# A Strassen down projection whose sums are handed out in quarters behind the next product's steps

## The chip, the core and the metric

The kernel runs on one NeuronCore of a Trainium2 chip. The metric is device time in microseconds (us) of one execution of the whole layer; the figure of a kernel is the median of its runs.

## The reference, cut to what matters

A bidirectional encoder layer (a state-space branch and a windowed attention branch, merged, then a squared-ReLU MLP) is applied to two sequences of 512 rows with 1024 columns, all in fp32. The change lies in the last line, in the second product:

```python
def encoder_layer(x, bias, ..., w_out, ln2, w_up, w_down):
    ...
    x = x + mixed @ w_out
    h2 = rms_norm(x, ln2)
    return x + jnp.square(jax.nn.relu(h2 @ w_up)) @ w_down     # (1024 x 4096) @ (4096 x 1024)
```

## The kernel before

The kernel runs its stages one after another: projections, state-space branch, attention, gating and output projection, then the MLP's up projection and its down projection. The last of these starts at about 1154 us of the profiled span and runs to the end.

**The seven products.** Activations and weights of the down projection are cut into 2 x 2 blocks and multiplied by Strassen's scheme, seven block products in place of eight. The up projection leaves the seven left operands (blocks, sums and differences of them) in a scratch tensor in DRAM, `a_scr`. The seven right operands are made on the fly from three sets of tiles: `k1`, `k2` and `k3`, each of eight tiles `k1_0` to `k1_7` and so on (128 partitions x 1024 values). Two sets are combined into one by a subtraction on VectorE (L1509) when a product needs a difference of weight blocks. The products run in the order 1, 5, 6, 3, 7, 2, 4.

**One product.** `product_d(n)` takes four PSUM banks (512 columns each, one for each 128 output rows) out of eight, and goes over the inner dimension in eight steps. In each step SyncE's queue loads a left tile `d_a` (three buffers); ScalarE rounds the two operands to a high part (`a_hi`, `b_hi`, L1514); VectorE takes the low parts (`a_lo`, `b_lo`, L1515); TensorE does 24 matmuls (`mm3`: high x high at L116, low x high at L117, high x low at L118, for 2 row blocks and 4 banks). The `hi` and `lo` tiles have two buffers each, so ScalarE may round a step's operands once TensorE is done with the step two before.

**The end of a product.** The four banks of a finished product are copied or added into accumulators in SBUF: `q1`, `q3`, `q4`, `q5`, each 4 x 512 columns, one quarter `q1[:, t]` for each bank. The residual `x` is read back from DRAM in tiles `xq` of 4 x 512 columns. There is one `xq` buffer, so each of its four loads (L1525, on SyncE's queue) waits until the last sum that reads the previous one is done. Finished quarters go to DRAM (`store`, L1530). After product 1, L1534 copies the banks to `q1` on ScalarE and L1536 adds `xq` to them in one instruction over all four quarters (128x2048). After product 5, L1540 copies the banks to `q5`, L1541 makes `q4` by quarters, and L1543 adds `xq` to all of `q5`. After product 7, L1555 and L1556 add by quarters, and L1558 adds `xq` to all of `q1`.

**What sets the order.** No order is written out by hand in this stage. A scheduler gives each engine a fixed sequence when the program is built: it goes by the order in which the code issues instructions, and lets a later one pass where its own estimate of the times says that an earlier one isn't ready. Each engine then works through its sequence strictly in order, waiting at semaphores.

Of the kernel before, what the change touches and what calls it, by code (L numbers as in the profile page):

```python
# [63 lines left out]
def hybrid_layer(ctx, tc, x, rel, onehot, w_qkv, w_ug, vectors, lam, coefs, w_glu, w_out, ln2,  # L64
                 w_up, w_down, out):
    nc = tc.nc
    V, S, PE, GP, SP = nc.vector, nc.scalar, nc.tensor, nc.gpsimd, nc.sync
# [18 lines left out]
    def sps():  # L86
        return ps_s.tile([P, 512], F32, tag="sps", name="sps")
# [26 lines left out]
    def mm3(ps, a, b, first, last):  # L114

        PE.matmul(ps, a[0], b[0], start=first, stop=False)  # L116
        PE.matmul(ps, a[0], b[1], start=False, stop=False)  # L117
        PE.matmul(ps, a[1], b[0], start=False, stop=last)  # L118
# [159 lines left out]
    with tc.tile_pool(name="xin", bufs=1, reuse_waits="tile") as xin, tc.tile_pool(name="ssmc", bufs=1) as sc:  # L278
# [148 lines left out]
        ps = ps_o.tile([P, 512], F32, tag="po", name="line")  # L427
# [21 lines left out]
    with tc.tile_pool(name="hst", bufs=1) as hp:  # L449
# [147 lines left out]
        with tc.tile_pool(name="ssmo", bufs=2) as sp:  # L597
# [46 lines left out]
            for q in range(GROUPS // SH):  # L644
# [7 lines left out]
                ps = sps()  # L652
# [91 lines left out]
    with tc.tile_pool(name="att", bufs=2, reuse_waits="tile") as ap, tc.tile_pool(name="attc", bufs=1, reuse_waits="tile") as ac:  # L744
# [293 lines left out]
        with tc.manual_schedule(engines={ET.PE, ET.Activation, ET.DVE, ET.Pool}):  # L1038
            for i, (j, sq) in enumerate(steps):
# [4 lines left out]
                for qb in range(NB):  # L1044
                    if 1 <= i < 3:
                        t = (i - 1) * NB + qb
# [366 lines left out]
    def bank():  # L1413
        return ps_m.tile([P, HALF], F32, tag="bank", name="bank")
# [69 lines left out]
    with tc.tile_pool(name="downb", bufs=1, side="right", reuse_waits="tile") as db, \  # L1484
            tc.tile_pool(name="down", bufs=2, side="right", reuse_waits="tile") as dp, \
            tc.tile_pool(name="down0", bufs=2, side="right", reuse_waits="tile") as d0, \
            tc.tile_pool(name="downc", bufs=1, reuse_waits="tile") as dc:

        q5 = db.tile([P, 4, HALF], F32, name="q5")
        db.tile([P, HALF * 2], F32, name="apart")  # L1490
        k1 = [(d0 if r < 3 else db).tile([P, 2, HALF], F32, name=f"k1_{r}", bufs=1) for r in range(NPAIR // 2)]
        k2, k3 = [[dc.tile([P, 2, HALF], F32, name=f"k{i}_{r}") for r in range(NPAIR // 2)] for i in (2, 3)]
        q1, q3, q4 = [dc.tile([P, 4, HALF], F32, name=f"q{i}") for i in (1, 3, 4)]

        def product_d(n):

            ps = [bank() for _ in range(4)]
            for r in range(0, NPAIR, 2):
                rs = slice(r, r + 2)
                a = d0.tile([P, 2, HALF], F32, tag="d_a", name="d_a", bufs=3)  # L1500
                SP.dma_start(a, a_scr[n - 1, :, rs, :])
                new = {1: (k1, 0, 0), 5: (k2, 0, 1), 6: (k3, 1, 1), 2: (k3, 1, 0)}.get(n)
                if new:
                    SP.dma_start(new[0][r // 2], w_down[new[1], new[2], :, rs, :])
                b = {1: k1, 5: k1, 6: k1, 3: k3, 7: k2, 2: k3, 4: k1}[n][r // 2]
                if n in (5, 6, 7, 4):

                    p, q = {5: (k2, k1), 6: (k3, k1), 7: (k3, k2), 4: (k1, k3)}[n]
                    V.tensor_sub(b, p[r // 2], q[r // 2])  # L1509
                hl = []  # L1510
                for src, tag in ((a, "a"), (b, "b")):
                    hi = (d0 if tag == "a" else dp).tile([P, 2, HALF], F32R, tag=tag + "_hi", name=tag + "_hi")
                    lo = dp.tile([P, 2, HALF], F32R, tag=tag + "_lo", name=tag + "_lo")
                    S.copy(hi, src)  # L1514
                    V.tensor_sub(lo, src, hi.bitcast(F32))  # L1515
                    hl.append((hi, lo))
                for rr in range(2):
                    for t in range(4):
                        mm3(ps[t], [q[:, rr, t * P:(t + 1) * P] for q in hl[0]], [q[:, rr, :] for q in hl[1]],
                            r + rr == 0, r + rr == NPAIR - 1)  # L1520
            return ps

        def residual(sq, c):
            xq = dp.tile([P, 4, HALF], F32, tag="xq", name="xq", bufs=1)
            SP.dma_start(xq, x1_scr[sq * HALF:(sq + 1) * HALF, c * HALF:(c + 1) * HALF].rearrange("(t p) n -> p t n", p=P))  # L1525
            return xq

        def store(src, t, sq, c):
            row = sq * HALF + t * P
            SP.dma_start(out[row:row + P, c * HALF:(c + 1) * HALF], src)  # L1530

        ps = product_d(1)
        for t in range(4):
            S.copy(q1[:, t], ps[t])  # L1534
        xq = residual(0, 0)
        V.tensor_add(q3, q1, xq)  # L1536
        xq = residual(0, 1)
        ps = product_d(5)
        for t in range(4):
            S.copy(q5[:, t], ps[t])  # L1540
            V.tensor_add(q4[:, t], q5[:, t], xq[:, t])  # L1541
        xq = residual(1, 1)
        V.tensor_add(q5, q5, xq)  # L1543
        ps = product_d(6)
        for t in range(4):
            V.tensor_add(q1[:, t], ps[t], q1[:, t])
            V.tensor_add(q4[:, t], q1[:, t], q4[:, t])
        ps = product_d(3)
        for t in range(4):
            V.tensor_add(q4[:, t], ps[t], q4[:, t])  # L1550
            store(q4[:, t], t, 0, 1)
        xq = residual(1, 0)
        ps = product_d(7)
        for t in range(4):
            V.tensor_add(q1[:, t], ps[t], q1[:, t])  # L1555
            V.tensor_add(q5[:, t], q5[:, t], q1[:, t])  # L1556
            store(q5[:, t], t, 1, 1)
        V.tensor_add(q1, q1, xq)  # L1558
        ps = product_d(2)
        for t in range(4):  # L1560
            V.tensor_add(q3[:, t], ps[t], q3[:, t])
            store(q3[:, t], t, 0, 0)
        ps = product_d(4)
        for t in range(4):
            V.tensor_sub(q1[:, t], q1[:, t], ps[t])
            store(q1[:, t], t, 1, 0)
# [79 lines left out]
```

## Time and profile before

| what | value |
|---|---|
| median of 3 runs | 1475.15 us (1472.97 to 1476.32) |
| span of the profiled execution, first to last instruction | 1471.1 us |
| median less that span | 4.0 us |
| TensorE busy | 1442.0 us, 98% of the span |
| VectorE busy | 1092.2 us, 74% |
| ScalarE busy | 754.9 us, 51% |
| down projection, from its first matmul | about 1154 us to the end |

The profiled execution's own time is its span of 1471.1 us and what lies around it; the runs' median lies 4.0 us above that span. Times inside the profile are counted from the first instruction. "Idle before" is the time that an engine stood still before an instruction, and the arrow behind it names what it waited for. A row that ends in "x3" is three like instructions in a row, with their time from the first's start to the last's end.

### The profile page before, as it was taken

To read this page: it belongs to the slowest core of one execution; us is meant where nothing else is said; L and a number is where in the kernel's file an instruction comes from. 1 tells how busy PE (TensorE), PEld (TensorE's weight loads), DVE (VectorE), ACT (ScalarE), POOL (GpSimd) and SP (SyncE) were. 2 spreads that over 40 slices of the span, in tenths; PEclk is the share of its full clock that TensorE was granted. 3 is DMA by queue.
4 is the path that set the end of the run, shared out by engine and by line. 5 is a ranking of instruction groups with operands and counts; after the bars stand their busy time and mean duration, and the time that the engine had idled before them with its cause. 6 is when DMAs were issued, how large, how long until landed. Compare 5 with 4: busy or idle time off the path is not lost.

```text
span 1471.1 us, 22069 instructions
## 1 busy us (share of the span) xinstructions
PE 1442.0 (98%) x8074; PEld 1230.7 (84%) x8074; DVE 1092.2 (74%) x1965; ACT 754.9 (51%) x1346; POOL 226.8 (15%) x372
## 2 busy tenths in 40 slices
PE   6999999999999999999999999999999999999998
PEld 4888888888999999987888878888888878888787
DVE  7989849995446899988985587777776597475553
ACT  6678852234336888786343355454454444333332
POOL 3044451003332442252100000000000000000000
PEclk9999999999999999999999999999999999999999
DMA  4455559428630533345552255444442993454441
GB/s 177 137 165 174 159 157 339 144 100 288 234 135 24 172 104 106 105 150 177 182 192 102 86 169 174 149 146 154 145 146 108 339 330 103 158 184 147 126 130 58
DMA packets 98269, 234.48 MB, mean 159 GB/s; under 512 B 11722, under 2 KB 23242, under 8 KB 98160
## 3 DMA queue, kind: packets, MB, share of 16 engines
q1 hardware_dynamic: 59088, 135.35, 28.5%
q0 software_dynamic: 15744, 47.23, 9.9%
q10 hardware_dynamic: 23328, 50.47, 9.4%
q8 instruction: 64, 1.05, 0.3%
q14 instruction: 45, 0.37, 0.1%
HBM read 163.78 MB, written 80.77 MB: 166 GB/s over the span
## 4 chain that ended last, share of the span: by engine, by line
PE 74%; DVE 12%; DMA 4%; issue 4%; ACT 4%; POOL 2%; SPq 0%; DVEq 0%; ACTq 0%; POOLq 0%
PE bank L117 14%; PE bank L118 13%; PE bank L116 13%; PE acc L185 6%; PE acc L821 5%; PE acc L117 3%; PE acc L118 3%; PE acc L116 3%; PE acc L123 2%; DMA c_raw<-in_w_ug_dram 2%; PE sps L553 2%; PE po L904 2%; PE sps L872 2%; PE tps L888 2%; PE acc L225 1%
## 5 line engine op out<-in xcount | busy, mean ns | idle before, releaser
L185 PE MATMUL acc<-act,c_hi 128*128 128x512 f32 x768 | 244.2, 396 | 1.0 <-DVE act L311 1.0
L117 PE MATMUL bank<-b_lo,a_hi 128*128 128x512 f32 x448 | 174.6, 390 | 2.3 <-DVE b_lo L1515 2.3
L118 PE MATMUL bank<-b_hi,a_lo 128*128 128x512 f32 x448 | 174.3, 389 | 0.0
L116 PE MATMUL bank<-b_hi,a_hi 128*128 128x512 f32 x448 | 173.5, 389 | 0.0
L185 PEld LDWEIGHTS acc<-act,c_hi 128*128 128x128 f32 x768 | 143.0, 189 | 30.4 <-DVE act L311 2.4
L1514 ACT CAST a_hi<-d_a 128x1024 fp32r<-128x1024 f32 x56 | 59.0, 1054 | 180.5 <-PE bank L117 177.1
L185 PE MATMUL acc<-act,c_lo 128*128 128x512 f32 x384 | 151.0, 393 | 0.0
L116 PE MATMUL bank<-act,act 128*128 128x512 f32 x368 | 143.3, 389 | 0.5 <-ACT f_sum L1339 0.5
L117 PE MATMUL bank<-act,act 128*128 128x512 f32 x368 | 143.3, 389 | 0.2 <-DVE act L1298 0.2
L118 PE MATMUL bank<-act,act 128*128 128x512 f32 x368 | 143.2, 389 | 0.0
L1515 DVE TENSOR_TENSOR a_lo<-d_a,a_hi 128x1024 fp32r<-128x1024 f32 x56 | 68.5, 1224 | 98.5 <-ACT a_hi L1514 98.5
L821 PE MATMUL acc<-w_hi,act 128*128 128x256 f32 x512 | 114.1, 291 | 0.0
L117 PEld LDWEIGHTS bank<-b_lo,a_hi 128*128 128x128 f32 x448 | 84.1, 188 | 20.7 <-DVE b_lo L1515 3.3
L116 PEld LDWEIGHTS bank<-b_hi,a_hi 128*128 128x128 f32 x448 | 84.1, 188 | 17.6
L118 PEld LDWEIGHTS bank<-b_hi,a_lo 128*128 128x128 f32 x448 | 84.1, 188 | 17.4
L821 PEld LDWEIGHTS acc<-w_hi,act 128*128 128x128 f32 x512 | 87.1, 190 | 3.7
L185 PEld LDWEIGHTS acc<-act,c_lo 128*128 128x128 f32 x384 | 72.3, 188 | 14.7 <-DVE c_lo L176 0.4
L882 ACT ACTIVATE p<-p,nmx 128x257 f32<-128x257 f32 (+1 forms) x128 | 72.1, 564 | 19.7 <-DVE nmx L876 17.6
L116 PEld LDWEIGHTS bank<-act,act 128*128 128x128 f32 x368 | 69.1, 188 | 15.4 <-ACT f_sum L1339 0.9
L117 PEld LDWEIGHTS bank<-act,act 128*128 128x128 f32 x368 | 69.1, 188 | 14.8 <-DVE act L1298 0.5
L123 PE MATMUL acc<-act,gc_hi 128*128 128x512 f32 x256 | 81.2, 394 | 0.0
L118 PEld LDWEIGHTS bank<-act,act 128*128 128x128 f32 x368 | 69.1, 188 | 14.2
(333 smaller groups left out, 3425.1 us busy)
## 6 DMA issues: line engine op xcount, KB each, us to landing
d_a<-a_scr SPq DMA_DIRECT2D x56, 512.0 KB, 3.8
raws<-in_w_up_dram SPq DMA_DIRECT2D x32, 512.0 KB, 4.0
a_scr<-t ACTq DMA_DIRECT2D x64, 256.0 KB, 2.9
k<-in_w_down_dram SPq DMA_DIRECT2D x32, 512.0 KB, 5.9
c_raw<-in_w_ug_dram SPq DMA_DIRECT2D x48, 256.0 KB, 3.8
ct_scr<-ctab POOLq DMA_DIRECT2D x16, 512.0 KB, 4.7
ctab_in<-ct_scr POOLq DMA_DIRECT2D x16, 512.0 KB, 7.3
a_scr<-a ACTq DMA_DIRECT2D x32, 256.0 KB, 2.0
```

What stands on the lines that cost most here:

```text
L116: PE.matmul(ps, a[0], b[0], start=first, stop=False)
L117: PE.matmul(ps, a[0], b[1], start=False, stop=False)
L118: PE.matmul(ps, a[1], b[0], start=False, stop=last)
L123: PE.matmul(ps, w[wi][:, k, :], rows[yi], start=k + p == 0, stop=k == KT - 1 and p == 2)
L185: PE.matmul(ps, w[wi][:, k, :], hT[s][hi][:, k, :], start=n == 0, stop=n == 3 * KT - 1)
L553: PE.matmul(ps[:, i * P:(i + 1) * P], bm[:, ri, g, :], u_sb[:, gp * SH + g, :], start=True, stop=True)
L821: PE.matmul(self.ps, hT[sq][act][:, k, col:col + P], w[:, k % 4, :], start=i == 0, stop=i == 3 * KT - 1)
L872: PE.matmul(ps[:, 0:self.nk], qs, kk[:, self.k0 * P:self.k1 * P], start=i == 0, stop=i == 1)
L882: S.activation(p, p, AF.Exp, bias=self.nmx[:, h:h + 1], scale=-1.0, accum_out=self.sums[:, h, self.qb:self.qb + 1])
L888: PE.transpose(pt[:, h * P:(h + 1) * P], self.p[:, h, 1 + i * P:1 + (i + 1) * P], ident)
L1514: S.copy(hi, src)
L1515: V.tensor_sub(lo, src, hi.bitcast(F32))
```

## The change

The sums, copies and stores that follow a product become a function of the quarter `t`, and four such pieces are put in a list, `waiting`. The next product works the list off: one piece behind the instructions of each of its first four steps (`settle(1)`), and whatever is left behind its last. The three sums over 128x2048 (L1536, L1543, L1558) become four sums over 128x512 each. The load of a residual is now issued in the code behind the whole of the product whose sums use it. The seventh product's sums stay as they were.

```diff
+        waiting = []
+
+        def settle(n):
+            for _ in range(min(n, len(waiting))):
+                waiting.pop(0)()
...
                         mm3(ps[t], [q[:, rr, t * P:(t + 1) * P] for q in hl[0]], [q[:, rr, :] for q in hl[1]],
                             r + rr == 0, r + rr == NPAIR - 1)
+                settle(1)
+            settle(len(waiting))
             return ps
...
-        ps = product_d(1)
-        for t in range(4):
-            S.copy(q1[:, t], ps[t])
-        xq = residual(0, 0)
-        V.tensor_add(q3, q1, xq)
-        xq = residual(0, 1)
-        ps = product_d(5)
...
-        V.tensor_add(q5, q5, xq)
...
-        V.tensor_add(q1, q1, xq)
...
+        def later(fn, *args):
+            for t in range(4):
+                waiting.append(lambda t=t: fn(t, *args))
+
+        def first_out(t, ps, xq):
+            S.copy(q1[:, t], ps[t])
+            V.tensor_add(q3[:, t], q1[:, t], xq[:, t])
+
+        def second_out(t, ps, xq):
+            S.copy(q5[:, t], ps[t])
+            V.tensor_add(q4[:, t], q5[:, t], xq[:, t])
+
+        def third_out(t, ps, xq):
+            V.tensor_add(q1[:, t], ps[t], q1[:, t])
+            V.tensor_add(q4[:, t], q1[:, t], q4[:, t])
+            V.tensor_add(q5[:, t], q5[:, t], xq[:, t])
+
+        def fourth_out(t, ps):
+            V.tensor_add(q4[:, t], ps[t], q4[:, t])
+            store(q4[:, t], t, 0, 1)
+
+        def fifth_out(t, ps, xq):
+            V.tensor_add(q1[:, t], ps[t], q1[:, t])
+            V.tensor_add(q5[:, t], q5[:, t], q1[:, t])
+            store(q5[:, t], t, 1, 1)
+            V.tensor_add(q1[:, t], q1[:, t], xq[:, t])
+
+        def sixth_out(t, ps):
+            V.tensor_add(q3[:, t], ps[t], q3[:, t])
+            store(q3[:, t], t, 0, 0)
+
+        later(first_out, product_d(1), residual(0, 0))
+        later(second_out, product_d(5), residual(0, 1))
+        later(third_out, product_d(6), residual(1, 1))
+        later(fourth_out, product_d(3))
+        later(fifth_out, product_d(7), residual(1, 0))
+        later(sixth_out, product_d(2))
         ps = product_d(4)
```

Since the scheduler sets the sequence, the built programs say what moved. VectorE's sequence differs at four places, the heads of products 5, 6, 3 and 2; ScalarE's at two (products 5 and 6), TensorE's at two (the second steps of products 5 and 2, where the first high x high matmuls change places with the others), and SyncE's at one. The head of product 7 (the sums of `q4`) and that of product 4 (the sums of `q3`) keep their rows. In the rows below the operands stand with their buffer numbers.

**Place A, the head of product 5 (after product 1).** VectorE before; the first two rows are the low parts of product 5's step 0, and `k1_1` is the right operand of step 1:

```order
L1515 TENSOR_TENSOR a_lo_12296<-d_a_12291,a_hi_12295 128x1024
L1515 TENSOR_TENSOR b_lo_12300<-k1_0_11967,b_hi_12299 128x1024
L1509 TENSOR_TENSOR k2_2_11977<-k3_2_11985,k2_2_11977 128x1024
L1509 TENSOR_TENSOR k1_0_11967<-k3_0_11983,k1_0_11967 128x1024
L1509 TENSOR_TENSOR k2_3_11978<-k3_3_11986,k2_3_11978 128x1024
L1515 TENSOR_TENSOR a_lo_12332<-d_a_12327,a_hi_12331 128x1024
L1536 TENSOR_TENSOR q3_11992<-q1_11991,xq_12282 128x2048
L1515 TENSOR_TENSOR b_lo_12336<-k1_1_11968,b_hi_12335 128x1024
```

VectorE now (a line's number is higher in the changed file: L1515 has become L1521, L1509 has become L1515, L1536 has become L1546):

```order
L1521 TENSOR_TENSOR a_lo_12289<-d_a_12284,a_hi_12288 128x1024
L1521 TENSOR_TENSOR b_lo_12293<-k1_0_11967,b_hi_12292 128x1024
L1515 TENSOR_TENSOR k2_2_11977<-k3_2_11985,k2_2_11977 128x1024
L1546 TENSOR_TENSOR q3_11992<-q1_11991,xq_12278 128x512 x3
L1515 TENSOR_TENSOR k1_0_11967<-k3_0_11983,k1_0_11967 128x1024
L1521 TENSOR_TENSOR a_lo_12327<-d_a_12322,a_hi_12326 128x1024
L1521 TENSOR_TENSOR b_lo_12331<-k1_1_11968,b_hi_12330 128x1024
L1546 TENSOR_TENSOR q3_11992<-q1_11991,xq_12278 128x512
L1515 TENSOR_TENSOR k1_1_11968<-k3_1_11984,k1_1_11968 128x1024
L1515 TENSOR_TENSOR k2_3_11978<-k3_3_11986,k2_3_11978 128x1024
L1521 TENSOR_TENSOR a_lo_12365<-d_a_12360,a_hi_12364 128x1024
L1521 TENSOR_TENSOR b_lo_12369<-k1_2_11969,b_hi_12368 128x1024
```

Between the low parts of step 0 and `b_lo` of step 1 stood three weight subtractions, `a_lo` and the whole sum; now there are two subtractions, three quarters of the sum and `a_lo`. The last quarter and the subtraction of `k2_3` stand behind `b_lo`.

**Place B, the head of product 2 (after product 7).** VectorE before; `b_lo_13485` belongs to step 0, `b_lo_13520` to step 1:

```order
L1515 TENSOR_TENSOR b_lo_13485<-k3_0_11983,b_hi_13484 128x1024
L1555 TENSOR_TENSOR q1_11991<-bank_13176,q1_11991 128x512
L1555 TENSOR_TENSOR q1_11991<-bank_13177,q1_11991 128x512
L1556 TENSOR_TENSOR q5_11965<-q5_11965,q1_11991 128x512 x2
L1555 TENSOR_TENSOR q1_11991<-bank_13178,q1_11991 128x512
L1555 TENSOR_TENSOR q1_11991<-bank_13179,q1_11991 128x512
L1556 TENSOR_TENSOR q5_11965<-q5_11965,q1_11991 128x512 x2
L1515 TENSOR_TENSOR a_lo_13516<-d_a_13512,a_hi_13515 128x1024
L1558 TENSOR_TENSOR q1_11991<-q1_11991,xq_13174 128x2048
L1515 TENSOR_TENSOR b_lo_13520<-k3_1_11984,b_hi_13519 128x1024
```

VectorE now (L1555, L1556 and L1558 have become L1562, L1563 and L1565):

```order
L1521 TENSOR_TENSOR b_lo_13478<-k3_0_11983,b_hi_13477 128x1024
L1562 TENSOR_TENSOR q1_11991<-bank_13172,q1_11991 128x512
L1562 TENSOR_TENSOR q1_11991<-bank_13173,q1_11991 128x512
L1563 TENSOR_TENSOR q5_11965<-q5_11965,q1_11991 128x512 x2
L1565 TENSOR_TENSOR q1_11991<-q1_11991,xq_13464 128x512
L1521 TENSOR_TENSOR a_lo_13513<-d_a_13509,a_hi_13512 128x1024
L1521 TENSOR_TENSOR b_lo_13517<-k3_1_11984,b_hi_13516 128x1024
L1565 TENSOR_TENSOR q1_11991<-q1_11991,xq_13464 128x512
L1562 TENSOR_TENSOR q1_11991<-bank_13174,q1_11991 128x512
L1562 TENSOR_TENSOR q1_11991<-bank_13175,q1_11991 128x512
L1563 TENSOR_TENSOR q5_11965<-q5_11965,q1_11991 128x512 x2
L1521 TENSOR_TENSOR a_lo_13552<-d_a_13548,a_hi_13551 128x1024
```

The low parts of step 1 have moved ahead of half of the sums and of three quarters of the one over `xq`.

**Place C, the head of product 6 (after product 5).** VectorE before; `xq_12285` is the second residual and `xq_12587` the third, which goes into the same buffer:

```order
L1541 TENSOR_TENSOR q4_11993<-q5_11965,xq_12285 128x512 x3
L1515 TENSOR_TENSOR a_lo_12635<-d_a_12630,a_hi_12634 128x1024
L1541 TENSOR_TENSOR q4_11993<-q5_11965,xq_12285 128x512
L1515 TENSOR_TENSOR b_lo_12639<-k1_1_11968,b_hi_12638 128x1024
L1515 TENSOR_TENSOR a_lo_12671<-d_a_12666,a_hi_12670 128x1024
L1515 TENSOR_TENSOR b_lo_12675<-k1_2_11969,b_hi_12674 128x1024
L1543 TENSOR_TENSOR q5_11965<-q5_11965,xq_12587 128x2048
L1515 TENSOR_TENSOR a_lo_12707<-d_a_12702,a_hi_12706 128x1024
```

VectorE now (L1541 and L1543 have become L1550 and L1555):

```order
L1550 TENSOR_TENSOR q4_11993<-q5_11965,xq_12580 128x512 x3
L1521 TENSOR_TENSOR a_lo_12629<-d_a_12624,a_hi_12628 128x1024
L1521 TENSOR_TENSOR b_lo_12633<-k1_1_11968,b_hi_12632 128x1024
L1550 TENSOR_TENSOR q4_11993<-q5_11965,xq_12580 128x512
L1521 TENSOR_TENSOR a_lo_12667<-d_a_12662,a_hi_12666 128x1024
L1521 TENSOR_TENSOR b_lo_12671<-k1_2_11969,b_hi_12670 128x1024
L1555 TENSOR_TENSOR q5_11965<-q5_11965,xq_12882 128x512 x4
L1521 TENSOR_TENSOR a_lo_12705<-d_a_12700,a_hi_12704 128x1024
```

The last reader of the second residual, a quarter of `q4`, has gone behind `b_lo` of step 1, and the sum over the third residual is four instructions where it was one. At places A and C ScalarE's fourth bank copy has likewise gone from between `a_hi` and `b_hi` of step 1 to behind `b_hi`. On SyncE's queue, at place B, the four stores of `q5` are now two and two, with one load of `d_a` between.

More of the change, by code (lines that the diff above doesn't have):

```diff
@@ L1530, in store @@
             SP.dma_start(out[row:row + P, c * HALF:(c + 1) * HALF], src)
-        ps = product_d(1)
-        for t in range(4):
+        def later(fn, *args):
+            for t in range(4):
+                waiting.append(lambda t=t: fn(t, *args))
+        def first_out(t, ps, xq):
             S.copy(q1[:, t], ps[t])
-        xq = residual(0, 0)
-        V.tensor_add(q3, q1, xq)
-        xq = residual(0, 1)
-        ps = product_d(5)
-        for t in range(4):
+            V.tensor_add(q3[:, t], q1[:, t], xq[:, t])
+        def second_out(t, ps, xq):
             S.copy(q5[:, t], ps[t])
             V.tensor_add(q4[:, t], q5[:, t], xq[:, t])
[L1542 to L1545, printed above, removed]
+        def third_out(t, ps, xq):
             V.tensor_add(q1[:, t], ps[t], q1[:, t])
             V.tensor_add(q4[:, t], q1[:, t], q4[:, t])
-        ps = product_d(3)
-        for t in range(4):
+            V.tensor_add(q5[:, t], q5[:, t], xq[:, t])
+        def fourth_out(t, ps):
             V.tensor_add(q4[:, t], ps[t], q4[:, t])
             store(q4[:, t], t, 0, 1)
-        xq = residual(1, 0)
-        ps = product_d(7)
-        for t in range(4):
+        def fifth_out(t, ps, xq):
             V.tensor_add(q1[:, t], ps[t], q1[:, t])
@@ L1557, in hybrid_layer @@
             store(q5[:, t], t, 1, 1)
-        V.tensor_add(q1, q1, xq)
-        ps = product_d(2)
-        for t in range(4):
+            V.tensor_add(q1[:, t], q1[:, t], xq[:, t])
+        def sixth_out(t, ps):
             V.tensor_add(q3[:, t], ps[t], q3[:, t])
             store(q3[:, t], t, 0, 0)
+        later(first_out, product_d(1), residual(0, 0))
[4 more added lines that the diff above has]
+        later(sixth_out, product_d(2))
         ps = product_d(4)
```

## The prediction

> **What bounds the kernel now.** I read the page's busy times first, then the waits of TensorE, then the instructions in order of time around each wait.
>
> ```profile
> span 1471.1 us, 22069 instructions
> PE 1442.0 (98%) x8074; PEld 1230.7 (84%) x8074; DVE 1092.2 (74%) x1965; ACT 754.9 (51%) x1346; POOL 226.8 (15%) x372
> PE bank L117 <- DVE b_lo L1515: 2.3, 2, 1.2
> ```
>
> TensorE (PE) is busy for 98% of the span, so only work that TensorE itself waits for can move the end. The third row is from the waits asked for the down projection alone (930 us to the end), and it is the only row there: two waits, both of a low x high matmul for a `b_lo` that VectorE (DVE) makes. Whatever the change does to sums and copies, it can win no more than these two stops cost.
>
> What they cost shows in TensorE's own instructions. A step of 24 matmuls, undisturbed, runs from the first row to the second; the rows from 1208.55 are step 1 of product 5 up to the start of its step 2; those from 1384.15 are step 1 of product 2 up to its step 2.
>
> ```profile
> 1203.11 0.39 PE L116 MATMUL bank<-b_hi,a_hi 128*128 128x512 f32 x1
> 1208.55 0.84 PE L116 MATMUL bank<-b_hi,a_hi 128*128 128x512 f32 x3
> 1210.53 0.50 PE L117 MATMUL bank<-b_lo,a_hi 128*128 128x512 f32 x1 [1.14 <-DVE b_lo L1515]
> 1215.46 0.39 PE L116 MATMUL bank<-b_hi,a_hi 128*128 128x512 f32 x1
> 1384.15 1.07 PE L116 MATMUL bank<-b_hi,a_hi 128*128 128x512 f32 x4
> 1386.37 0.50 PE L117 MATMUL bank<-b_lo,a_hi 128*128 128x512 f32 x1 [1.15 <-DVE b_lo L1515]
> 1391.04 0.39 PE L116 MATMUL bank<-b_hi,a_hi 128*128 128x512 f32 x1
> ```
>
> A step takes 1208.55 - 1203.11 = 5.44 us, or 0.227 us for one matmul. The first disturbed step takes 6.91 and loses 1.47 us, the second takes 6.89 and loses 1.45. Together that is 2.92 us, more than the 2.3 of idle time, since a refilled pipeline is slow for one or two matmuls: at the first stop the fourth matmul was due at 1208.55 + 3 x 0.227 = 9.23 and came at 10.53, 1.30 late, so 0.17 of its 1.47 is refill.
>
> **The change part by part.** *Place A, the head of product 5.* Here are VectorE's rows before (DVE), then ScalarE's (ACT).
>
> ```profile
> 1201.38 1.22 DVE L1515 TENSOR_TENSOR b_lo<-k,b_hi 128x1024 fp32r<-128x1024 f32 x1
> 1202.51 3.49 DVE L1509 TENSOR_TENSOR k<-k,k 128x1024 f32<-128x1024 f32 x3
> 1205.92 1.22 DVE L1515 TENSOR_TENSOR a_lo<-d_a,a_hi 128x1024 fp32r<-128x1024 f32 x1
> 1207.05 2.28 DVE L1536 TENSOR_TENSOR q<-q,xq 128x2048 f32<-128x2048 f32 x1
> 1209.26 1.22 DVE L1515 TENSOR_TENSOR b_lo<-k,b_hi 128x1024 fp32r<-128x1024 f32 x1
> 1210.39 1.22 DVE L1509 TENSOR_TENSOR k<-k,k 128x1024 f32<-128x1024 f32 x1
> ...
> 1201.27 1.95 ACT L1534 COPY q<-bank 128x512 f32<-128x512 f32 x3 [1.62 <-PE bank L118]
> 1203.11 1.05 ACT L1514 CAST a_hi<-d_a 128x1024 fp32r<-128x1024 f32 x1
> 1204.06 0.58 ACT L1534 COPY q<-bank 128x512 f32<-128x512 f32 x1
> 1204.54 1.07 ACT L1514 CAST b_hi<-k 128x1024 fp32r<-128x1024 f32 x1
> ```
>
> The reader should see that from 1201.38 VectorE has no gap: this stop is VectorE's queue, five instructions long, and not ScalarE, whose `b_hi` was done at 1205.61. From start to start an instruction of 1024 columns takes 1.13 us and that of 2048 takes 2.21. A sum of 512 columns takes 0.60, from the two rows of L1555 and L1556 in place B below (1379.36 to 1380.56 to 1381.76, two instructions each).
>
> Now the same with the new order. Starting at 1202.51: `k2_2` 1.13, three quarters of `q3` 1.80, `k1_0` 1.13, `a_lo` 1.13; `b_lo` starts at 1207.70, ends 1.22 later at 1208.92, and with the 0.05 that lay before from its end (1210.48) to the matmul (1210.53) TensorE has it at 1208.97. ScalarE doesn't hold this up: the three copies are done at 1203.22, and the new order casts `b_hi` straight behind `a_hi`, half a microsecond sooner; the fourth copy slips to about 1205.6, and its quarter of `q3` isn't wanted before 1208.84. TensorE's sequence now puts one high x high matmul ahead of the first low x high, which is due at 1208.55 + 0.23 = 1208.78. So 0.19 is still late, with at most 0.17 of refill: 0.36 stays, and this place wins 1.11. Bounds: nothing stays (win 1.47), or the sums don't overlap at all and each takes its whole 0.69 (the L1541 row below), three times 0.09 more, so 0.63 stays (win 0.84). I take 0.36, from two consecutive sums on the same engine.
>
> The removed stop was also VectorE's time to catch up, so I followed its queue for three more steps. Step 2 has one quarter, `k1_1`, `k2_3`, `a_lo` before `b_lo`: 1208.84 + 0.60 + 3 x 1.13 = 1212.83, ready at 1214.10, wanted at 1214.58 (step 2 now starts at 1214.35). Step 3 has `k2_4`, `k1_2`, `k2_5`, `a_lo`: `b_lo` starts at 1218.48, ready at 1219.75, wanted at 1220.02. Step 4, with `k2_7` behind it now, is ready at 1224.3 and wanted at 1225.5. So there is no new stop, but at step 3 the margin is 0.27; if it fails, it costs what is missing and no more.
>
> *Place B, the head of product 2.* VectorE, then ScalarE, before:
>
> ```profile
> 1376.87 1.37 DVE L1555 TENSOR_TENSOR q<-bank,q 128x512 f32<-128x512 f32 x2 [0.18 <-PE bank L118]
> 1378.15 1.29 DVE L1556 TENSOR_TENSOR q<-q,q 128x512 f32<-128x512 f32 x2
> 1379.36 1.28 DVE L1555 TENSOR_TENSOR q<-bank,q 128x512 f32<-128x512 f32 x2
> 1380.56 1.29 DVE L1556 TENSOR_TENSOR q<-q,q 128x512 f32<-128x512 f32 x2
> 1381.76 1.22 DVE L1515 TENSOR_TENSOR a_lo<-d_a,a_hi 128x1024 fp32r<-128x1024 f32 x1
> 1382.89 2.29 DVE L1558 TENSOR_TENSOR q<-q,xq 128x2048 f32<-128x2048 f32 x1
> 1385.09 1.22 DVE L1515 TENSOR_TENSOR b_lo<-k,b_hi 128x1024 fp32r<-128x1024 f32 x1
> ...
> 1378.68 1.05 ACT L1514 CAST a_hi<-d_a 128x1024 fp32r<-128x1024 f32 x1 [3.43 <-PE bank L117]
> 1379.64 1.04 ACT L1514 CAST b_hi<-k 128x1024 fp32r<-128x1024 f32 x1
> 1384.12 1.06 ACT L1514 CAST a_hi<-d_a 128x1024 fp32r<-128x1024 f32 x1 [3.44 <-PE bank L117]
> ```
>
> Now two sums of L1555, two of L1556 and one quarter come first: 1379.36 + 0.60 = 1379.96; `a_hi` is there (1379.73). `a_lo` runs to 1381.09, `b_lo` is done by 1382.31, and TensorE wants it at 1384.15 + 0.23 = 1384.38: two microseconds to spare, so the whole 1.45 goes. What is late next? The deferred sums: one quarter, two of L1555, two of L1556, to 1385.2, behind them `a_lo` and `b_lo` of step 2, done by 1387.6, wanted at 1384.15 + 5.44 + 0.23 = 1389.8. The banks of product 7 come free by 1384.0 instead of 1380.6, but only product 4 wants them, a product later. On SyncE's queue the loads of `d_a` behind the last two stores of `q5` wait for sums that end at 1385.2; the first of them would wait in any case for its buffer, which `a_lo` of step 2 frees at about 1386.4. All of this costs nothing, with over 2 us of cover.
>
> *Place C, the head of product 6.* There was no stop here, and one could come:
>
> ```profile
> 1250.33 0.69 DVE L1541 TENSOR_TENSOR q<-q,xq 128x512 f32<-128x512 f32 x1
> 1250.93 1.22 DVE L1515 TENSOR_TENSOR b_lo<-k,b_hi 128x1024 fp32r<-128x1024 f32 x1
> 1258.34 2.29 DVE L1543 TENSOR_TENSOR q<-q,xq 128x2048 f32<-128x2048 f32 x1 [1.38 <-DMA xq<-x_scr]
> 1251.05 0.37 SPq L1525 DMA_DIRECT2D xq<-x_scr  x1
> 1264.42 0.39 PE L116 MATMUL bank<-b_hi,a_hi 128*128 128x512 f32 x1
> 1264.65 0.39 PE L117 MATMUL bank<-b_lo,a_hi 128*128 128x512 f32 x1
> DMA to landing us min/median/max: 5.1/6.3/7.2
> ```
>
> The load of the third residual is issued (1251.05) when the last quarter of `q4` (1250.33) is done, and VectorE stood 1.38 for its landing at 1258.3. The quarter now stands behind `b_lo`, 1.13 later: issue at 1252.18, landing at 1259.5 if it takes as long again. Four sums take 2.40 where one took 2.21: 1261.9. `a_lo` and `b_lo` of step 3 follow: ready at 1264.25, wanted at 1264.65 (second matmul of that step). The margin is 0.40, with the longest of the four landings (last row) in the sum; the median would add 0.9. Cost taken: nothing; bounds 0 and 0.5.
>
> *The rest.* The heads of products 7 and 4 and the tail of the kernel keep their order, and in product 3 `b_lo` of step 1 only moves ahead of three sums where there was no stop: nothing. Nine more VectorE instructions are in the sums above.
>
> Sum: -1.11 - 1.45 = -2.56 us against the span of 1471.1, and the same against the median of 1475.15, since what lies outside the span isn't touched: 1472.6 us.
>
> One rule speaks against this. The Trainium skill, "VectorE: DVE Perf Modes" (its errata section), gives an fp32 tensor_tensor a fixed part of 151 cycles, so 691 ns at 512 columns and 2291 at 2048, and tells to avoid many small tiles; the section "The DRAIN you can't avoid" says that the next one starts only when the pipe is empty. The single rows agree (0.69, 2.28), the starts don't: 0.60 apart. By that rule 0.63 would stay at place A, and the sum would be -2.29, or 1472.9.
>
> **The rivals.** *All of both stops goes, and a little luck with it.* For it: 0.19 late at place A is little beside a chain of five durations, and `b_hi` comes sooner. Against: nothing else in this stage can be won, so -2.92, 1472.2 us, is the end of it. That is 0.198% of 1475.15, and about 0.2% (2.95 us) is what a measurement of this kernel can tell from no change: it would be counted as faster only by the scatter of the runs, of which those before lie up to 2.2 below and 1.2 above their median. The forecast itself, 0.4 short of that line, has the same luck to hope for.
>
> *No change: the stops come back elsewhere.* VectorE has the same work and a little more, and 0.27 of margin at step 3 of product 5. For it: there it runs without a gap over four steps. Against: what is moved out (a quarter and `k2_3` at A, `k2_7` past step 4) meets steps with slack, and place B has two microseconds. To give back all needs 2.56 at place A, more than its whole stop. 1475.2 us.
>
> *Slower: the third residual at place C.* VectorE's sequence is fixed, so `a_lo` and `b_lo` of step 3 stand behind the sum over `xq`. Once the landing takes over 7.3 + 0.4 = 7.7 us from issue, each microsecond stops TensorE for one. At 10.3 the gain is gone, at 13.2 the kernel is slower by 0.2%: 1478.1 us. Against: none of the four landings took over 7.2, and the load is now further from the `d_a` load ahead of it.
>
> **How the numbers follow.** Forecast of a gain between 2.0 and 2.8: 0.66. All of both stops: 0.18. Given back in part or whole: 0.12. Slower by place C or something unseen: 0.04. By the line of 0.2%: the forecast stands 0.4 us inside it, and medians of three runs that scatter over 3.4 us (the 2.2 and 1.2 above) may differ by a microsecond for no cause, my estimate; so about 4 in 10 of it and half of the second case would be read as faster; a few of the third case too by scatter. That makes 0.38 faster, 0.58 same, 0.04 slower. The likeliest case has 1471.6 to 1473.6 as its own range. The range of the time: low is 1472.2 less the 2.2 by which the runs before scatter downward, 1470.0; high is nothing won, 1475.2.
>
> **What would show it.** In the trace after: no wait of L117 for `b_lo` at place B, and one of 0.2 to 0.4 us or none at A; step 1 of product 5 in 5.4 to 6.1 us; `b_lo` of its step 3 ready just before its matmul; the sum over the third residual at about 1258.4 (the times behind A come 1.1 sooner). I am wrong if TensorE waits at steps 2 or 3 of product 5, at step 3 of product 6, or anywhere that it didn't before, or if the two waits are gone and the span hasn't shrunk by them.

## The result: both stops go as worked out, 0.18% faster, from a lower base than the forecast had

| | kernel before | changed kernel |
|---|---|---|
| median, 22 runs each | 1472.47 us (1469.15 to 1476.35) | 1469.18 us (1467.16 to 1475.95) |
| profiled execution: own time, span | 1472.97, 1471.1 us | 1471.94, 1470.2 us |
| first to last matmul of the down projection | 307.42 us | 304.92 us |

The ratio of the runs is 0.9982, with a 95% interval from 0.9974 to 0.9989: 2.65 us less, between 1.6 and 3.8 (the two medians lie 3.29 apart). The forecast was 2.56 less, a ratio of 0.9983. Its absolute number, 1472.6 us, and its range down to 1470.0 miss the measured 1469.18, and that error lies in the base from which the gain was subtracted (below).

The spans of the two profiles differ by 0.9 us only, and the stage by 2.50, since the stage began later in the second one. The rows are the stage's first and last matmul, before and then after (start, duration, instruction):

```profile
1159.55 0.39 PE L116 MATMUL bank<-b_hi,a_hi 128*128 128x512 f32 x1
1466.97 0.39 PE L118 MATMUL bank<-b_hi,a_lo 128*128 128x512 f32 x1
```

```profile
1161.08 0.39 PE L116 MATMUL bank<-b_hi,a_hi 128*128 128x512 f32 x1
1466.00 0.39 PE L118 MATMUL bank<-b_hi,a_lo 128*128 128x512 f32 x1
```

(The stage's first matmul is at 1159.55 in the profile before; the 1154 given in the description of the kernel was too early.) I call the difference of two such rows the stage. Back to back its 1343 starts at 0.2267 us would be 304.5.

TensorE's waits, asked for from 930 us on, have no row at all in the changed kernel, but a very short wait isn't listed. Its own instructions at place A (step 1 of product 5, and the start of step 2) and at place B (the starts of steps 1 and 2 of product 2) say how much is left:

```profile
1210.12 0.39 PE L116 MATMUL bank<-b_hi,a_hi 128*128 128x512 f32 x1
1210.61 0.50 PE L117 MATMUL bank<-b_lo,a_hi 128*128 128x512 f32 x1
1215.96 0.39 PE L116 MATMUL bank<-b_hi,a_hi 128*128 128x512 f32 x1
...
1383.95 0.39 PE L116 MATMUL bank<-b_hi,a_hi 128*128 128x512 f32 x1
1389.39 0.39 PE L116 MATMUL bank<-b_hi,a_hi 128*128 128x512 f32 x1
```

At A the second matmul starts 0.49 us after the first and not 0.23, and the step takes 5.84 us instead of 5.44: it loses 0.40, where it lost 1.47; at B it takes 5.44 and loses nothing, where it lost 1.45. VectorE's rows show why. At A (first six rows) the three quarters and `k1_0` stand ahead of `b_lo`, which starts 1.14 after `a_lo` and not 3.34 after it; at B (next four) `a_lo` and `b_lo` come ahead of half of the sums; at C (last three) the sum waits for the residual.

```profile
1202.99 1.22 DVE L1521 TENSOR_TENSOR b_lo<-k,b_hi 128x1024 fp32r<-128x1024 f32 x1
1204.12 1.22 DVE L1515 TENSOR_TENSOR k<-k,k 128x1024 f32<-128x1024 f32 x1
1205.26 1.89 DVE L1546 TENSOR_TENSOR q<-q,xq 128x512 f32<-128x512 f32 x3
1207.07 1.22 DVE L1515 TENSOR_TENSOR k<-k,k 128x1024 f32<-128x1024 f32 x1
1208.20 1.22 DVE L1521 TENSOR_TENSOR a_lo<-d_a,a_hi 128x1024 fp32r<-128x1024 f32 x1
1209.34 1.22 DVE L1521 TENSOR_TENSOR b_lo<-k,b_hi 128x1024 fp32r<-128x1024 f32 x1
...
1379.84 0.68 DVE L1565 TENSOR_TENSOR q<-q,xq 128x512 f32<-128x512 f32 x1
1380.44 1.22 DVE L1521 TENSOR_TENSOR a_lo<-d_a,a_hi 128x1024 fp32r<-128x1024 f32 x1
1381.58 1.22 DVE L1521 TENSOR_TENSOR b_lo<-k,b_hi 128x1024 fp32r<-128x1024 f32 x1
1382.71 0.68 DVE L1565 TENSOR_TENSOR q<-q,xq 128x512 f32<-128x512 f32 x1
...
1259.67 2.50 DVE L1555 TENSOR_TENSOR q<-q,xq 128x512 f32<-128x512 f32 x4 [2.18 <-DMA xq<-x_scr]
1262.09 1.22 DVE L1521 TENSOR_TENSOR a_lo<-d_a,a_hi 128x1024 fp32r<-128x1024 f32 x1
1263.22 1.22 DVE L1521 TENSOR_TENSOR b_lo<-k,b_hi 128x1024 fp32r<-128x1024 f32 x1
```

### The profile page after: what moved, and what is told of

It reads as the page before. It is cut to its first block, busy times and chain, and to the rows that moved or that the text cites. A ratio compares the mean times of both kernels' runs of the same rounds, so it can differ in the third digit from the quotient of the medians.

```text
span 1470.2 us, 22081 instructions
## 1 busy us (share of the span) xinstructions
PE 1442.4 (98%) x8074; PEld 1231.2 (84%) x8074; DVE 1092.7 (74%) x1974; ACT 755.0 (51%) x1346; POOL 226.9 (15%) x372
## 3 DMA queue, kind: packets, MB, share of 16 engines
q8 instruction: 64, 1.05, 0.3%
## 4 chain that ended last, share of the span: by engine, by line
PE 72%; DVE 14%; DMA 4%; issue 4%; ACT 3%; POOL 2%; SPq 0%; DVEq 0%; ACTq 0%; POOLq 0%
PE bank L117 13%; PE bank L118 13%; PE bank L116 13%; PE acc L185 6%; PE acc L821 5%; PE acc L117 3%; PE acc L118 3%; PE acc L116 3%; PE acc L123 2%; PE sps L553 2%; PE po L904 2%; DMA c_raw<-in_w_ug_dram 2%; PE sps L872 2%; PE tps L888 2%; DVE t L621 1%
## 5 line engine op out<-in xcount | busy, mean ns | idle before, releaser
L1521 DVE TENSOR_TENSOR a_lo<-d_a,a_hi 128x1024 fp32r<-128x1024 f32 x56 | 68.5, 1223 | 96.3 <-ACT a_hi L1520 96.3
```

## The experiments

Theory: the gain is the two stops of TensorE, and each is VectorE's queue in front of one `b_lo`. Rivals: the spreading as a whole (banks, loads, the other four heads), or a scatter of the stops. Each run is one profiled execution; the two that were timed as well are said to be. "Lead" is the time from the end of VectorE's `b_lo` of step 0 of product 5 to TensorE's first matmul of that step; "lost" is what the step takes above 5.44 us.

| kernel | stage | lead before A | lost at A | lead + lost | lost at B |
|---|---|---|---|---|---|
| before | 307.42 | 0.51 | 1.47 | 1.98 | 1.45 |
| before, again | 308.60 | 0.36 | 1.58 | 1.94 | 1.48 |
| only A spread | 306.41 | 0.38 | 0.48 | 0.86 | 1.48 |
| only B spread | 306.63 | 0.09 | 1.86 | 1.95 | 0 |
| all but A and B spread | 307.53 | 0.33 | 1.63 | 1.96 | 1.48 |
| changed | 304.92 | 0.47 | 0.40 | 0.87 | 0 |
| changed, again | 305.20 | 0.12 | 0.78 | 0.90 | 0 |
| changed, in the code's order (twice) | 304.41, 304.41 | | 0 | | 0 |

**Before, again.** No edit.

> The kernel before once more, unchanged, for a second profile. Measured is the stage length: from the first matmul of the down projection to its last, which was 307.42 us in the first profile of before and 304.92 in that of the changed kernel; back to back it would be 1343 x 0.2267 = 304.5. Theory (two stops of TensorE, 1.47 and 1.45 us, and nothing else in this stage): 307.4 again, within 0.1, and the start of the stage anywhere within some 2 us of 1159.5, since the scatter of the runs lies ahead of it. Rival (the stops themselves vary from run to run, so that one profile proved little): another length, by 0.5 us or more.

The stage took 308.60, not 307.4, so the rival has a point: the stops vary. Steps 4 and 5 of product 1 lost 1.08 us here, where the first profile lost 0.03, and A lost 1.58. B was as before. Ahead of the low parts of step 4 of product 1 VectorE has a subtraction that, by the built program, is for product 5, and it stood for the weight tile; the rows are from the first profile and from this one:

```profile
1177.65 1.23 DVE L1509 TENSOR_TENSOR k<-k,k 128x1024 f32<-128x1024 f32 x1 [3.80 <-DMA k<-in_w_down_dram]
1178.94 1.23 DVE L1509 TENSOR_TENSOR k<-k,k 128x1024 f32<-128x1024 f32 x1 [4.86 <-DMA k<-in_w_down_dram]
```

It stood 1.06 us longer, and product 1 lost 1.05 more.

**Only A spread.**

```diff
-        ps = product_d(1)
-        for t in range(4):
-            S.copy(q1[:, t], ps[t])
-        xq = residual(0, 0)
-        V.tensor_add(q3, q1, xq)
+        later(first_out, product_d(1), residual(0, 0))
```

> Only the sums after product 1 are handed out in quarters (place A); all others as before. Theory: the stop at step 1 of product 5 falls from 1.47 to 0.40 us, the one at product 2 stays at 1.45, the stage takes 306.35 us (306.2 to 306.5). Rival one (it is the whole spreading, the loads and the banks that win, no single place): 307.4, or some even part of the 2.5. Rival two (A is enough, the second stop was a result of the first): 304.9.

306.41: A falls to 0.48, B stays. Both rivals fall. The two waits, one row each:

```profile
1210.81 0.50 PE L117 MATMUL bank<-b_lo,a_hi 128*128 128x512 f32 x1 [0.19 <-DVE b_lo L1521]
1387.04 0.50 PE L117 MATMUL bank<-b_lo,a_hi 128*128 128x512 f32 x1 [1.15 <-DVE b_lo L1521]
```

**Only B spread.**

```diff
-        xq = residual(1, 0)
-        ps = product_d(7)
...
-        V.tensor_add(q1, q1, xq)
+        later(fifth_out, product_d(7), residual(1, 0))
```

> Only the sums after product 7 are handed out in quarters (place B); all others as before. Theory: the stop at step 1 of product 2 is gone, the one at product 5 stays at 1.47, the stage takes 307.42 - 1.45 = 305.97 us (305.8 to 306.1). Rival one (no single place wins): 307.4 or an even part. Rival two (deferred sums come back as a new stop at step 2 or 3 of product 2): above 306.5.

B is gone, and nothing came in its place, as the theory has it. The stage of 306.63 is outside what I gave, because A, left as it was, lost 1.86 instead of 1.47 and product 1 lost 0.32. It is the row of A that moved:

```profile
1206.61 0.50 PE L117 MATMUL bank<-b_lo,a_hi 128*128 128x512 f32 x1 [1.56 <-DVE b_lo L1521]
```

The table's fifth column settles what moves it. Lead and loss add up to 1.94 to 1.98 in each kernel that sums in one block at A, and to 0.86 to 0.90 in each that spreads: A's loss is a fixed queue less VectorE's lead, and the change wins about 1.08 us whatever the lead is. (From `b_lo` of step 0 to that of step 1 VectorE's queue is 1.53 us shorter, 6.35 for 7.88, but TensorE now asks for the second two matmuls, 0.45 us, sooner.) The lead shrinks when VectorE stands for weight tiles in front of place A. Here is the weight subtraction ahead of A in three traces (the profile before, that of the changed kernel, that with only B spread); the last number is how long VectorE stood for the load:

```profile
1196.83 3.50 DVE L1509 TENSOR_TENSOR k<-k,k 128x1024 f32<-128x1024 f32 x3 [1.18 <-DMA k<-in_w_down_dram]
```

```profile
1198.44 3.50 DVE L1515 TENSOR_TENSOR k<-k,k 128x1024 f32<-128x1024 f32 x3 [1.23 <-DMA k<-in_w_down_dram]
```

```profile
1192.91 3.50 DVE L1515 TENSOR_TENSOR k<-k,k 128x1024 f32<-128x1024 f32 x3 [1.61 <-DMA k<-in_w_down_dram]
```

This wait and the lead add up to 1.69 or 1.70 us in all seven profiles of the table that keep the scheduler's order: what VectorE stands there, it lacks at A. By the built program the first of these three subtractions makes `k2_0` for product 7; the scheduler has put it in front of the low parts of product 5, and so its wait for a load, early work for product 7, holds up the low parts that TensorE needs next.

**All but A and B spread.**

```diff
+        later(second_out, product_d(5), residual(0, 1))
+        later(third_out, product_d(6), residual(1, 1))
+        later(fourth_out, product_d(3))
...
+        later(sixth_out, product_d(2))
```

> The complement: places A and B as before, the sums after products 5, 6, 3 and 2 handed out in quarters. Theory: both stops stay, the rest wins and costs nothing, 307.4 us (307.3 to 307.6). Rival one (the other four are part of the gain): below 307.0. Rival two (the later load of the third residual costs something at step 3 of product 6): above 307.8, with a wait there.

307.53, with both waits in place and no other step that lost time: the other four heads neither win nor cost.

**Twice the block at B.** On the kernel before:

```diff
         V.tensor_add(q1, q1, xq)
+        for h in (0, 2):
+            V.tensor_add(apart, q5[:, h:h + 2], xq[:, h:h + 2])
```

> The kernel before, with two more VectorE sums of 1024 columns (into a tile that nobody reads) beside the sum over the last residual at place B; both stand ahead of b_lo of step 1, and TensorE's sequence is the same as before. Theory (each microsecond of VectorE's queue ahead of that b_lo beyond the margin is a microsecond of TensorE): 2 x 1.13 = 2.27 more, a loss at that step of 3.7 instead of 1.45, the stage 309.7 us (309.4 to 309.9). Rival (the stop is set by something else, a bank or a load, and VectorE just ends at about the same time): 307.4 to 308.5.

`b_lo` was done 4.43 us after the step's start instead of 2.16: exactly the 2.27 added. But the step lost 5.24 instead of 1.45, 1.5 more than the delay, and the stage took 311.71, above what I gave (A and product 1 lost 0.3 and 0.2 more than in the first profile). The rows are the stop and what follows it; then the windows around it, whose column before the last two is the granted clock of TensorE:

```profile
1385.50 1.07 PE L116 MATMUL bank<-b_hi,a_hi 128*128 128x512 f32 x4
1389.99 0.80 PE L117 MATMUL bank<-b_lo,a_hi 128*128 128x512 f32 x1 [3.42 <-DVE b_lo L1515]
1391.01 0.63 PE L117 MATMUL bank<-b_lo,a_hi 128*128 128x512 f32 x1
1391.43 0.63 PE L118 MATMUL bank<-b_hi,a_lo 128*128 128x512 f32 x1
1393.42 0.39 PE L116 MATMUL bank<-b_hi,a_hi 128*128 128x512 f32 x1
```

```profile
1384.00:1388.00 4.00, 2.56 (x12) 1.79 (x10) 4.00 (x4) 2.00 (x2) 0.00 (x0) 1.00 0.21 80
1388.00:1392.00 4.00, 2.01 (x5) 1.63 (x6) 4.00 (x4) 0.00 (x0) 0.00 (x0) 0.73 0.45 131
1392.00:1396.00 4.00, 4.00 (x17) 3.20 (x16) 0.20 (x1) 0.00 (x0) 0.00 (x0) 0.84 0.44 131
```

After 3.42 us of idleness the matmuls came 0.43 us apart instead of 0.227, for about 3 us, and the granted clock was 0.73 and 0.84. The stops of 1.14 us in the kernel before had no such tail. The Trainium skill, "TensorE: Matmul & The Clock Gate" (Part 1), says that the array's clock is halved after an idle window of about 3.4 us and comes back after as long a busy one; this trace agrees, with 3.42 and about 3. But the length of a stop alone doesn't settle it. Two waits of TensorE for a table ahead of the stage, one in the profile before and one in the timed run of the code's order (below), show that:

```profile
385.30 0.46 PE L655 MATMUL sps<-u_sb,toep 128*128 128x128 f32 x2 [2.15 <-DMA toep<-toep_scr]
386.42 0.46 PE L655 MATMUL sps<-u_sb,toep 128*128 128x128 f32 x2 [2.62 <-DMA toep<-toep_scr]
```

Behind the first the granted clock was 0.51 from 386.0 to 389.4 us; behind the second, the longer one, it stayed at 1.00.

**Two more sums at C.**

```diff
         def third_out(t, ps, xq):
+            if t == 0:
+                for h in (0, 2):
+                    V.tensor_add(apart, q3[:, h:h + 2], xq[:, h:h + 2])
```

> The changed kernel, with two more VectorE sums of 1024 columns (into a tile that nobody reads) among the sums over the third residual at place C. By the built sequence 2 x 1.13 + 2 x 0.60 = 3.47 us now stand between the residual's landing and a_lo of step 3, where 4 x 0.60 = 2.40 stood: 1.07 more, against a margin of 0.68 us in the changed kernel's trace (b_lo of step 3 done at 1264.44, wanted at 1265.18, 0.05 to hand over). Theory: step 3 of product 6 loses about 0.4 plus up to 0.17 of refill, the stage takes 305.3 to 305.5 us. Rival one (there is more cover than I count): 304.9. Rival two (the load itself gets later, or the delay is passed on to later steps): above 306.

```profile
1256.79 1.23 DVE L1555 TENSOR_TENSOR apart<-q,xq 128x1024 f32<-128x1024 f32 x1 [1.81 <-DMA xq<-x_scr]
1260.27 1.22 DVE L1521 TENSOR_TENSOR a_lo<-d_a,a_hi 128x1024 fp32r<-128x1024 f32 x1
1261.41 1.22 DVE L1521 TENSOR_TENSOR b_lo<-k,b_hi 128x1024 fp32r<-128x1024 f32 x1
1262.68 0.50 PE L117 MATMUL bank<-b_lo,a_hi 128*128 128x512 f32 x1
```

From landing to `a_lo` there are 3.48 us, as counted. The residual landed 6.59 us after its issue this time instead of 6.96, so `b_lo` came at the very moment it was wanted, and the step lost 0.18: less than I gave. The stage of 305.82 is above my range for another reason, A's leftover of 0.88 and 0.24 in product 1. The count of VectorE's queue at C holds; a delay beyond a few tenths there was not run.

**The weight subtractions for product 7 on GpSimd.**

```diff
-                    V.tensor_sub(b, p[r // 2], q[r // 2])
+                    (GP if n == 7 else V).tensor_sub(b, p[r // 2], q[r // 2])
```

> The changed kernel, with the eight weight subtractions for product 7 (k2 from k3 and k2) on GpSimd instead of VectorE; the scheduler puts them on VectorE early in products 1 and 5, far ahead of their use. Theory (place A is VectorE's queue, and what is left of its stop is the one subtraction of k2_2 in it): b_lo of step 1 is ready 1.13 us sooner, the remaining 0.40 goes, and the stage takes 304.5 us (304.4 to 304.6). Rival (the two engines get in each other's way, and VectorE's instructions take longer while GpSimd subtracts): durations above 1.22 for 1024 columns and a stage of 305 or more.

```profile
1200.62 23.95 POOL L1515 TENSOR_TENSOR k<-k,k 128x1024 f32<-128x1024 f32 x8 [341.62 <-DMA k<-in_w_down_dram]
1207.48 3.31 DVE L1515 TENSOR_TENSOR k<-k,k 128x1024 f32<-128x1024 f32 x1
1210.71 8.38 DVE L1546 TENSOR_TENSOR q<-q,xq 128x512 f32<-128x512 f32 x3
1222.29 3.36 DVE L1521 TENSOR_TENSOR b_lo<-k,b_hi 128x1024 fp32r<-128x1024 f32 x1
1227.31 1.21 DVE L1521 TENSOR_TENSOR a_lo<-d_a,a_hi 128x1024 fp32r<-128x1024 f32 x1
```

The rival came true: the stage took 320.64. While GpSimd subtracted, 3.0 us for each of the eight, an instruction of VectorE with 1024 columns took 3.3 us instead of 1.22, and a sum of 512 columns 2.8; once GpSimd was done, 1.21 again. The step at A lost 14.1 us. The Trainium skill, "SBUF — State Buffer" (SBUF: two separate sides), calls the port pair that the two engines share an exclusive lock, held for a whole instruction, also by a VectorE instruction with two SBUF inputs; the durations, one GpSimd instruction for each of VectorE's, agree. Whether A's leftover is the subtraction in VectorE's queue, this run can't say; the next one bears on it.

**The code's order.** The changed kernel, with VectorE and ScalarE taken out of the scheduler's hands in this stage:

```diff
-            tc.tile_pool(name="downc", bufs=1, reuse_waits="tile") as dc:
+            tc.tile_pool(name="downc", bufs=1, reuse_waits="tile") as dc, \
+            tc.manual_schedule(engines={ET.DVE, ET.Activation}):
```

> The changed kernel, with the sequence of VectorE and ScalarE in this stage as the code issues it, one piece behind each step, instead of the scheduler's. Theory: a step then has at most 3 x 1.13 of low parts and weight subtraction, or 2 x 1.13 and three sums of 0.60, for VectorE, 4.1 us of the 5.44 that TensorE takes, so no stop is left and the stage takes 304.5 us (304.4 to 304.6). Rival one (the scheduler's running ahead was needed somewhere, say at the start of product 1 or 5, where weight tiles arrive late): a new wait, and above 304.9. Rival two (the rest at A is no queue but a fixed cost of the product's change): 304.9.

304.41 us, no wait in the stage: TensorE ran back to back, so what was left at A is VectorE's queue and no fixed cost of a new product. VectorE now has gaps ahead of each step's low parts, where it waits for ScalarE:

```profile
1202.95 1.22 DVE L1516 TENSOR_TENSOR k<-k,k 128x1024 f32<-128x1024 f32 x1
1204.66 1.23 DVE L1522 TENSOR_TENSOR a_lo<-d_a,a_hi 128x1024 fp32r<-128x1024 f32 x1 [0.49 <-ACT a_hi L1521]
1205.81 1.22 DVE L1522 TENSOR_TENSOR b_lo<-k,b_hi 128x1024 fp32r<-128x1024 f32 x1
1206.94 0.69 DVE L1547 TENSOR_TENSOR q<-q,xq 128x512 f32<-128x512 f32 x1
1207.54 1.22 DVE L1516 TENSOR_TENSOR k<-k,k 128x1024 f32<-128x1024 f32 x1
1210.10 1.23 DVE L1522 TENSOR_TENSOR a_lo<-d_a,a_hi 128x1024 fp32r<-128x1024 f32 x1 [1.34 <-ACT a_hi L1521]
```

It was timed beside the changed kernel, 12 runs each against 23 of before.

> The changed kernel with VectorE's and ScalarE's sequence as the code issues it, a second time and timed. Its first profile had a stage of 304.41 us and no wait in it, against 307.42 and 308.60 in two of the kernel before and 304.92 in that of the changed kernel. Theory (the leftovers of place A vary with the landing of the weight tiles that VectorE waits for, and by hand it doesn't wait for them there): 304.4 again, to a tenth, whatever the start of the stage; against before a ratio of about 0.9976 (3.0 to 4.2 us less). Rival (the clean stage was luck of one run): a stage of 304.8 or more.

> The changed kernel once more, timed beside the hand-ordered one on the same chip. Theory: stage between 304.9 and 305.8, the difference being the leftover of place A (0.40 to 0.88 us so far) and up to 0.3 in steps 4 and 5 of product 1; a ratio of about 0.9982 to before, and 0.5 to 1.0 us behind the hand-ordered kernel, which this timing can't tell from nothing. Rival (place A is settled at 0.40): 304.9 within 0.1.

In the code's order: stage 304.41 again, median 1469.03 us, ratio 0.9982 (0.9973 to 0.9991), where I gave about 0.9976. Changed kernel: stage 305.20 with 0.78 left at A, median 1469.45, ratio 0.9983 (0.9972 to 0.9994). By the stage the first is 0.5 to 0.8 us shorter; the times can't tell the two apart.

**The old code in the code's order.** The same edit on the kernel before, with its sums in one block.

> The kernel before, its sums in one block at the end of each product, but with VectorE's and ScalarE's sequence as the code issues it, so that nothing of the next product passes the sums. Theory (the scheduler had hidden nearly all of these sums already, and the change could only win what it had left): a stop at each of the six heads, from the end of the product to the first b_lo: 5 to 10 us for each, about 15 after product 5 where the single residual buffer is loaded in between (7 us), 49 us together, and some 1.5 us more for each since TensorE's records showed a lower clock after a stop of 3.4 us in the kernel with two more sums: a stage of 350 to 370 us. Rival (the scheduler's order hides little, the sums are short): below 330.

```profile
PE bank L116 <- ACT b_hi L1515: 22.4, 4, 11.0
PE bank L117 <- DVE b_lo L1516: 12.0, 2, 7.1
```

A stage of 352.43 us, inside what I gave; the heads lost 5.0 to 9.8 us each and 13.7 after product 5. The waits (us in total, times, longest) are 34.4, and refill and slow clock bring the loss to 48. The block of sums is worth that much where nothing passes it, and the scheduler had hidden all but 2.9 of it.

## Why the prediction was right and wrong

**Wrong: the base.** The term of the sum that failed is the first one, 1475.15; the gain behind it was right. I put the gain against the median of three runs and took the 4.0 us between that and the span as what lies outside the span. Only 1.8 of it does: in every profile here whose own time is known it is 1.7 to 1.9 (1474.33 against 1472.5 in the second one of before), and of the three runs only the one of 1472.97 fits the profiled span of 1471.1. The other 2.2 was the three runs' luck; over 22 runs the kernel's median is 1472.47, 2.7 below the term. From the profiled execution's own time the same sum gives 1470.4; from the 22-run median, 1469.9 against a measured 1469.18. So of the 3.4 us by which 1472.6 was too high, 2.7 are the base; the other 0.7 lies within the interval of the gain. The lower bound, 1470.0, was set by the scatter about the wrong middle as well.

**Where the scatter lies.** Ahead of the stage: its first matmul came between 1154.9 (the kernel with only B spread) and 1161.8 us (that with GpSimd), with the same instructions up to there in all of them. One of the waits that differ is TensorE's for a table from DRAM, before and then with only B spread (us in total, times, longest):

```profile
PE sps L655 <- DMA toep<-toep_scr: 2.9, 2, 2.1
```

```profile
PE sps L655 <- DMA toep<-toep_scr: 0.9, 2, 0.6
```

The clock goes with it: between 380 and 396 us the granted clock was 0.79 or 0.89 in the nine profiles whose stage began at 1159.55 or later, and 1.00 in the four whose stage began sooner.

**Right: place A** wins 1.07 us between the first two profiles, and 1.08 on average by the table's fifth column (predicted 1.11). `b_lo` of step 1 starts 6.35 after `b_lo` of step 0; I had 6.32. The sums' 0.60 from start to start held (1.89 us for three), so the version by 0.69 each falls. What I had not seen is that A's loss is no constant: I took VectorE's start at 1201.38 for given, and it hangs on a load. That 0.40 stayed where I had 0.36 is partly luck, since the lead was nearly the same in those two profiles (0.51 and 0.47); in two later runs of the same sequence at A 0.78 and 0.88 stayed, above my bound of 0.63.

**Right: place B** wins all of its 1.45 to 1.48, and deferred sums cost nothing at steps 2 and 3. **Right: the following steps of product 5**: `b_lo` of step 3 had 0.21 us left where I had 0.27. **Place C**: margin 0.68 where I had 0.40, because the residual landed in 7.0 and not 7.3 us. That margin is thin: in the second profile of the changed kernel the residual took 7.4 us and 0.23 was left. **The rest**: zero, as the complement shows. Neither the rival of no change nor that of the late residual came, and not all of both stops went.

## What to carry to other kernels

The gain of rearranging hidden work is bounded by the stops of the bounding engine, and those can be read to a tenth of a microsecond: add them up first, then follow the queue in front of each. Set the sum against many runs, not against a median of three; the profiled execution's own time is one draw from the same scatter (1469.15 to 1476.35 us here). And see what the scheduler made of a change in the code: it had already hidden 45 of 48 us, it undid part of the spreading, and what was left came from early work for later products, which waits for its loads in front of what is needed now.

## What the runs showed of the hardware that I had not expected

A stop of 3.42 us cost about 1.5 us more than itself, with the granted clock down to 0.73 behind it; one of 1.14 us cost no more than the refill. A stop of 2.15 us was followed by a lower clock too, one of 2.62 us was not. Eight subtractions on the idle GpSimd, which took 24 us there, made VectorE's instructions nearly three times as long and the stage 16 us longer than that of the changed kernel.
